# Forming the token-shifted inputs on two engines, and those of the second stream inside its low-rank loop

## The chip, the cores and the metric

The kernel runs on one core of a Trainium2 chip. A core has engines that run side by side, each in the order of its own queue: the matrix engine TensorE (PE in the profile), VectorE (DVE), ScalarE (ACT), GpSimd (POOL) and SyncE (SP), which here issues most of the DMAs. The metric is device microseconds (us) of one execution, as the median of several runs; a change is judged by the ratio of the two kernels' times.

## The reference

Two layers are applied to two streams of 512 tokens by 1024 features, with shared weights: first an RWKV-7 block (a linear recurrence, run forward and backward), then neighbourhood attention on a grid. The change touches the inputs of the first block. Cut to that:

```
xx = 0.5 * (x_prev + x_next) - xn            # tokens t-1 and t+1, zeros at the ends
lerp = lambda j: xn + xx * mu[j]
r, k, v = lerp(0) @ w_r, lerp(1) @ w_k, lerp(2) @ w_v
z = xn @ w_z
for d in range(2):
    w_log = -softplus(-(w0[d] + tanh(lerp(3 + d) @ w1[d]) @ w2[d])) - 0.5
    a = sigmoid(a0[d] + (lerp(5 + d) @ a1[d]) @ a2[d])
    ...                                      # scan of direction d with r, k, v, w_log, a
```

The matrices w1 and a1 have 64 columns each, so four narrow products of 1024 x 64 stand beside the wide ones. Everything is fp32.

## The kernel before

Activations lie transposed: 128 features on the partitions, 512 tokens along them, so one stream is KT = 8 tiles of 128x512. A fp32 matrix product is made of three matmuls on rounded halves: each operand is split into `hi` (a cast on ACT) and `lo` (a subtraction on DVE), by `halves`, L377 and L378, and `gemm` issues hi·hi, hi·lo and lo·hi for each of 8 tiles (L428 to L430). A column is 128 output features: 24 matmuls, after which ACT evicts the sum.

Work is in two parts. In the prelude, up to about 170 us, the code of `prelude(0)`, `prelude(1)` and the columns of z and k of stream 0 is interleaved, and a scheduler with its own estimates of durations sets the order of instructions on every engine. From then on (`scan_phase`), orders come from a planner written for this kernel, which puts instructions down one after another: weights of further columns are split at L730 and L732, their products are L811 to L813, and the low-rank weights and gates of the scan are prepared (L863 to L904) for the scans themselves. On every engine instructions run in their order, and a waiting one holds up those behind it.

What `prelude(s)` does for a stream: loads the eight tiles, makes their sum of squares, the reciprocal root (`rstds`, L461 to L470, with a matmul against ones that spreads it over the partitions) and the normed tiles `xn`. Then it forms `xx` in two DVE instructions for each tile, L541 and L542. The loop over k at L549 to L561 multiplies the normed tiles with the four narrow matrices, as they stand (`ps`) and multiplied by their mu (`pm`), twelve matmuls a tile (L558 to L560); the shift by a token is made afterwards on the small products (L569 to L579), which become four hidden activations (L581, of 64 rows: two with tanh). For stream 0 they stay on the chip; for stream 1 each is saved to memory (`save("hid")`). The tiles `lm` and `lr` of that part have a single buffer each. After it come the shifted inputs, a lerp by one DVE instruction a tile: v of stream 0, and k, r and v of stream 1, 32 tiles in all at L590, each saved to memory for later columns. They use the pool tag "ls" with four buffers, as do `hi` and `lo` of stream 1 in the loop over k. The inputs k and r of stream 0 are made by `shifted` (L608, 16 tiles) and split at once for the columns.

`save` (L327) and `load` (L333) both issue on SP in this part. Memory tensors are named in the orders by a leading d: dlk, dlr and dlv are shifted inputs, dhid hidden activations, dss the sums of squares of k, which are saved, loaded in another shape and made into the factors drn (L669 to L672). `rb` and `k` are the first tiles of the scan's preparation, loaded on SP; L863 on DVE multiplies them, L865 and L867 split the low-rank weights, and L882 on PE is the first product with these. `cv` holds the given vectors, `dv` vectors derived from them once, at the start, in `consts`.

Of the kernel before, what the change touches and what calls it, by code (L numbers as in the profile page):

```python
# [11 lines left out]
F32 = mybir.dt.float32  # L12
F32R = mybir.dt.float32r
AF = mybir.ActivationFunctionType
ALU = mybir.AluOpType
# [4 lines left out]
P = 128  # L20
T = 512
# [210 lines left out]
class Trunk:  # L232
# [110 lines left out]
    def consts(self):  # L343
        nc, cp = self.nc, self.cp
        self.cc = cp.tile([P, NCC], F32, tag="cc", name="cc")
        nc.sync.dma_start(self.cc, self.a["const"])
        c = lambda n, w: self.cc[:, CC[n]:CC[n] + w]
        self.ident, self.bones, self.ssel = c("ident", 128), c("bones", 128), c("ssel", 2)
        if self.SUMS:
            self.bones = cp.tile([P, 128], F32R, tag="sel", name="sel")  # L350
            nc.scalar.copy(self.bones, c("bones", 128))
        self.mstrict, self.mr = c("mstrict", 64), (c("mr", 64), self.cc[:, CC["mr"] + 64:CC["mr"] + 128])
        self.scan = (c("scan", T), self.cc[:, CC["scan"] + 1:CC["scan"] + 1 + T])
        w = c("win", 64)
        self.lower = bass.AP(tensor=w.tensor, offset=w.offset + 31, ap=[list(w.ap[0]), [-1, 32], [1, 32]])
        self.ones = cp.tile([P, P], F32, tag="ones", name="ones")
        nc.vector.memset(self.ones, 1.0)
        self.one = self.ones[:, 0:1]
        self.dv = dv = cp.tile([P, 88], F32, tag="dv", name="dv")
        v = lambda n, w, o=0: self.cv[:, CV[n] + o:CV[n] + o + w]  # L360
        ts = nc.vector.tensor_scalar
        ts(dv[:, 0:32], v("w0", 32), 0.5, None, op0=ALU.mult)
        ts(dv[:, 32:40], v("ka", 8), 0.5, None, op0=ALU.mult)
        ts(dv[:, 40:48], v("ka", 8), -0.5, 1.0, op0=ALU.mult, op1=ALU.add)
        ts(dv[:, 48:56], v("bin", 8), 0.125, None, op0=ALU.mult)
        ts(dv[:, 56:64], v("bin", 8, 24), 0.5, None, op0=ALU.mult)
        ts(dv[:, 64:72], v("bin", 8, 16), 0.5, None, op0=ALU.mult)
        ts(dv[:, 72:80], v("lnw", 8), 0.5, None, op0=ALU.mult)
        ts(dv[:, 80:88], v("lnb", 8), 0.5, None, op0=ALU.mult)

    def vec(self, n, i):
        return self.cv[:, CV[n] + i:CV[n] + i + 1]
# [127 lines left out]
    def prelude(self, s):  # L500
        nc = self.nc
        vt, gps, act = nc.vector, nc.gpsimd, nc.scalar
# [3 lines left out]
        for k in range(KT):  # L506
            if s == 0 and k == self.WFIRST:
                self.first = [self.weight(self.a["w_z"][0])]
            t = self.t("xn", (P, T + 2), 16, F32, self.lp)
# [21 lines left out]
        xn, xx = [], []  # L531
        for k, t in enumerate(xs):
            x = t[:, 1:T + 1]
# [5 lines left out]
        for k, t in enumerate(xs):  # L539
            u = self.t("xx", (P, T), 16, F32, self.lp)  # L540
            vt.tensor_tensor(u, t[:, 2:T + 2], t[:, 0:T], op=ALU.add)  # L541
            vt.scalar_tensor_tensor(u, u, 0.5, t[:, 1:T + 1], op0=ALU.mult, op1=ALU.subtract)  # L542
            xx.append(u)
            yield
        self.shift[s] = xn, xx

        pm = self.p("pf", (P, 2, T))
        ps = (self.p("pm"), self.p("us"))
        for k in range(KT):  # L549
            if s == 0:  # L550
                hi, lo = self.xz[k]
            else:
                hi, lo = (self.t("ls", (P, T), 4, F32R, self.lp) for _ in range(2))
                self.halves(xn[k], lo, hi, self.alt(k))
            for q2 in range(2):
                for out, w in ((pm[:, q2], self.wm), (ps[q2], self.wl)):
                    a, b = (m[:, k % 4] for m in w[2 * q2 + k // 4])
                    nc.tensor.matmul(out, a, hi, start=(k == 0), stop=False)  # L558
                    nc.tensor.matmul(out, a, lo, start=False, stop=False)
                    nc.tensor.matmul(out, b, hi, start=False, stop=(k == KT - 1))  # L560
                yield  # L561
        for q2 in range(2):
            mw = self.t("lm", (P, KT * P), 1, F32, self.lp)[:, 0:T + 2]
            lr = self.t("lr", (P, KT * P), 1, F32, self.lp)
            y, u = lr[:, 0:T], lr[0:64, T:2 * T]
# [18 lines left out]
                else:  # L584
                    self.save("hid", s, q, u)
            yield
        for kind, j in (("v", 2),) if s == 0 else (("k", 1), ("r", 0), ("v", 2)):
            for k in range(KT):
                t = self.t("ls", (P, T), 4, F32, self.lp)
                vt.scalar_tensor_tensor(t, xx[k], self.vec("mu", 8 * j + k), xn[k], op0=ALU.mult, op1=ALU.add)  # L590
                self.save("l" + kind, s, k, t)
                yield
        if s == 1:
            for k in range(KT):
# [2 lines left out]
    def hidden(self, q, u):  # L597
# [2 lines left out]
        self.nc.scalar.copy(h[0:64], u)  # L600
        self.nc.vector.tensor_tensor(h[64:128], u, h[0:64].bitcast(F32), op=ALU.subtract)

    def shifted(self, s, j):
        xn, xx = self.shift[s]

        def source(k):
            t = self.t("xr", bufs=self.NXR)
            self.nc.vector.scalar_tensor_tensor(t, xx[k], self.vec("mu", 8 * j + k), xn[k], op0=ALU.mult, op1=ALU.add)  # L608
            return t

        return self.operands(source)
# [1305 lines left out]
```

## Time and profile before

| | |
|---|---|
| median of 3 runs | 1658.08 us (1657.85 to 1667.48) |
| the profiled execution | 1657.03 us, span 1655.2 us |
| mean granted clock of PE | 0.974 |
| DVE instructions L542, busy | 10.0 us |
| DVE lerps L590 and L608, busy | 23.3 and 12.0 us |

A line of a group gives the line in the code, engine and operation, output and inputs, shape and count, then busy time and mean duration of one, then the engine's idle time just before them and what ended it. A line of the timeline gives the start and the duration in us; what stands in square brackets is the time that the engine had been idle and what ended that. A line of the waits gives the engine, the instruction, what it waited for, and the sum, the number and the longest of such waits. "zy", "pm", "pf" and "us" are accumulators of PE; "whi" and "wlo" halves of weights, "act" halves of inputs.

### The profile page before, as it was taken

To read this page: it belongs to the slowest core of one execution; us is meant where nothing else is said; L and a number is where in the kernel's file an instruction comes from. 1 tells how busy PE (TensorE), PEld (TensorE's weight loads), DVE (VectorE), ACT (ScalarE), POOL (GpSimd) and SP (SyncE) were. 2 spreads that over 40 slices of the span, in tenths; PEclk is the share of its full clock that TensorE was granted. 3 is DMA by queue.
4 is the path that set the end of the run, shared out by engine and by line. 5 is a ranking of instruction groups with operands and counts; after the bars stand their busy time and mean duration, and the time that the engine had idled before them with its cause. 6 is when DMAs were issued, how large, how long until landed. Compare 5 with 4: busy or idle time off the path is not lost.

```text
span 1655.2 us, 46478 instructions
## 1 busy us (share of the span) xinstructions
PE 1559.5 (94%) x18826; PEld 1197.2 (72%) x18826; DVE 1225.7 (74%) x2725; ACT 983.8 (59%) x1979; POOL 175.7 (11%) x334
## 2 busy tenths in 40 slices
PE   7989899998989998998988999999999999999998
PEld 6867667776667776776766777777777788777776
DVE  8995669688789787897888897865576585665564
ACT  5443566766756677665575665454567665455562
POOL 0000113311101224010000011000000002100000
PEclk9989999999999999999997999999999999999999
DMA  6435678776676787676777675554865346755553
GB/s 212 159 127 171 209 239 280 221 246 218 229 259 228 219 261 242 211 253 187 236 229 233 193 254 162 190 180 133 281 218 171 109 141 210 245 157 181 167 157 108
DMA packets 176312, 336.28 MB, mean 203 GB/s; under 512 B 20929, under 2 KB 53825, under 8 KB 176097
## 3 DMA queue, kind: packets, MB, share of 16 engines
q1 hardware_dynamic: 152800, 253.60, 48.2%
q0 software_dynamic: 23296, 79.71, 14.1%
q8 instruction: 148, 2.42, 0.6%
q14 instruction: 68, 0.55, 0.1%
HBM read 227.71 MB, written 105.51 MB: 201 GB/s over the span
## 4 chain that ended last, share of the span: by engine, by line
PE 49%; DVE 7%; ACT 5%; DMA 3%; issue 3%; POOL 0%; DVEq 0%; SPq 0%; ACTq 0%; POOLq 0%
PE pg L428 6%; PE pg L429 6%; PE pg L430 6%; PE pm L811 4%; PE pm L812 3%; PE pm L813 3%; PE sc L1437 2%; PE po L1470 2%; PE pf L1099 2%; PE pt L1455 2%; PE us L1218 1%; PE zy L1171 1%; PE us L1198 1%; PE zy L1222 1%; DVE ab L925 1%
## 5 line engine op out<-in xcount | busy, mean ns | idle before, releaser
L811 PE MATMUL pm<-act,whi 128*128 128x512 f32 x640 | 286.4, 447 | 12.2 <-ACT whi L730 4.9
L812 PE MATMUL pm<-act,whi 128*128 128x512 f32 x640 | 258.0, 403 | 10.2 <-DVE act L758 5.1
L813 PE MATMUL pm<-act,wlo 128*128 128x512 f32 x640 | 257.1, 402 | 6.0 <-DVE wlo L732 6.0
L811 PEld LDWEIGHTS pm<-act,whi 128*128 128x128 f32 x640 | 123.2, 192 | 55.3 <-issue 10.4
L377 ACT CAST whi<-raw 128x512 fp32r<-128x512 f32 x148 | 91.5, 618 | 118.3 <-PE pg L429 64.7
L428 PE MATMUL pg<-act,whi 128*128 128x512 f32 x384 | 158.5, 413 | 0.4 <-DVE tmp L1393 0.4
L429 PE MATMUL pg<-act,whi 128*128 128x512 f32 x384 | 152.5, 397 | 0.0
L430 PE MATMUL pg<-act,wlo 128*128 128x512 f32 x384 | 152.2, 396 | 0.0
L812 PEld LDWEIGHTS pm<-act,whi 128*128 128x128 f32 x640 | 123.8, 193 | 36.1 <-DVE act L758 14.9
L813 PEld LDWEIGHTS pm<-act,wlo 128*128 128x128 f32 x640 | 123.3, 193 | 36.0 <-DVE wlo L732 9.0
L378 DVE TENSOR_TENSOR wlo<-raw,whi 128x512 fp32r<-128x512 f32 x148 | 101.6, 688 | 58.8 <-ACT whi L377 56.5
L732 DVE TENSOR_TENSOR wlo<-raw,whi 128x512 fp32r<-128x512 f32 x160 | 109.1, 685 | 36.4 <-ACT whi L730 36.1
L730 ACT CAST whi<-raw 128x512 fp32r<-128x512 f32 x160 | 98.0, 617 | 41.2 <-PE pm L812 21.8
L428 PEld LDWEIGHTS pg<-act,whi 128*128 128x128 f32 x384 | 72.3, 188 | 15.6 <-issue 3.3
L430 PEld LDWEIGHTS pg<-act,wlo 128*128 128x128 f32 x384 | 72.3, 188 | 14.9 <-issue 0.3
L429 PEld LDWEIGHTS pg<-act,whi 128*128 128x128 f32 x384 | 72.4, 189 | 13.9 <-issue 2.5
L1003 DVE TENSOR_TENSOR etmp<-N 128x30 f32<-128x30 f32 (+14 forms) x240 | 78.6, 328 | 4.3
L1005 DVE TENSOR_TENSOR N<-etmp,N 128x30 f32<-128x30 f32 (+14 forms) x240 | 78.8, 328 | 4.0
L1448 DVE CUSTOM_DVE_ANT_0 sb<-sc,bias 128x256 f32<-128x256 f32 x128 | 49.2, 419 | 28.0 <-PE pt L1455 20.4
L1451 ACT ACTIVATE sb<-sb,mx 128x256 f32<-128x256 f32 x128 | 64.0, 502 | 6.8 <-DVE mx L1450 6.5
L1099 PE MATMUL pf<-cab 64*64 64x128 f32 (+1 forms) x2048 | 66.2, 266 | 0.4 <-issue 0.3
L1210 ACT COPY X<-us 64x256 f32<-64x256 f32 x128 | 46.9, 366 | 26.2 <-PE zy L1077 22.2
(403 smaller groups left out, 3636.2 us busy)
## 6 DMA issues: line engine op xcount, KB each, us to landing
dab<-ab POOLq DMA_DIRECT2D x32, 1024.0 KB, 7.1
cab<-dab SPq DMA_DIRECT2D x64, 512.0 KB
raw<-in_w_in_dram SPq DMA_DIRECT2D x128, 256.0 KB
bias<-in_rpb_dram SPq DMA_DIRECT2D x32, 384.0 KB
raw<-in_w_z_dram SPq DMA_DIRECT2D x32, 256.0 KB
raw<-in_w_k_dram SPq DMA_DIRECT2D x32, 256.0 KB
raw<-in_w_r_dram SPq DMA_DIRECT2D x32, 256.0 KB
k<-dk SPq DMA_DIRECT2D x32, 256.0 KB
```

The lines of the kernel that those rows point to most:

```text
L377: self.nc.scalar.copy(hi, src)
L378: (eng or self.nc.vector).tensor_tensor(lo, src, hi.bitcast(F32), op=ALU.subtract)
L428: nc.tensor.matmul(ps, hi, x[k][0], start=(k == 0), stop=False)
L429: nc.tensor.matmul(ps, hi, x[k][1], start=False, stop=False)
L430: self.mm = nc.tensor.matmul(ps, lo, x[k][0], start=False, stop=(k == KT - 1))
L730: nc.scalar.copy(hi, raw[h])
L732: nc.vector.tensor_tensor(lo, raw.pop(h), hi.bitcast(F32), op=ALU.subtract)
L811: nc.tensor.matmul(ps, hi[:, at], xh, start=(k == 0), stop=False)
L812: nc.tensor.matmul(ps, hi[:, at], xl, start=False, stop=False)
L813: nc.tensor.matmul(ps, lo[:, at], xh, start=False, stop=(k == KT - 1))
L1005: vt.tensor_tensor(N[:, q + 1:, :q], tv, N[:, q + 1:, :q], op=ALU.add)
L1099: end = nc.tensor.matmul(st.f[half(a), h, 0, d, g] if st.last else st.f[half(a), h, :, d, g], ab[half(h), d, g, 2 * e[d] + 1 - a], rt if s ...
```

## The change

Three things are done. L542 goes, so that `xx` is the plain sum of the neighbours. The lerp, xn + mu (0.5 sum - xn), is written as (1 - mu) xn + (0.5 mu) sum: ACT multiplies xn by a scale for each partition (1 - mu), and DVE adds the sum times 0.5 mu, in a new function `lerp` that all 48 tiles use. The factors are two more derived vectors. And the 24 shifted inputs of stream 1 are formed inside the loop of the narrow products, three after the products of each tile, where they stood after the hidden activations.

```
+        ts(dv[:, 88:112], v("mu", 24), 0.5, None, op0=ALU.mult)
+        ts(dv[:, 112:136], v("mu", 24), -1.0, 1.0, op0=ALU.mult, op1=ALU.add)
...
             vt.tensor_tensor(u, t[:, 2:T + 2], t[:, 0:T], op=ALU.add)
-            vt.scalar_tensor_tensor(u, u, 0.5, t[:, 1:T + 1], op0=ALU.mult, op1=ALU.subtract)
...
+        def mixed(kind, j, k):
+
+            t = self.t("ls", (P, T), 4, F32, self.lp)
+            self.lerp(t, xn[k], xx[k], 8 * j + k)
+            self.save("l" + kind, s, k, t)
...
                     nc.tensor.matmul(out, b, hi, start=False, stop=(k == KT - 1))
+                yield
+            for kind, j in (("k", 1), ("r", 0), ("v", 2)) if s else ():
+                mixed(kind, j, k)
                 yield
...
-        for kind, j in (("v", 2),) if s == 0 else (("k", 1), ("r", 0), ("v", 2)):
+        if s == 0:
             for k in range(KT):
-                t = self.t("ls", (P, T), 4, F32, self.lp)
-                vt.scalar_tensor_tensor(t, xx[k], self.vec("mu", 8 * j + k), xn[k], op0=ALU.mult, op1=ALU.add)
-                self.save("l" + kind, s, k, t)
+                mixed("v", 2, k)
                 yield
...
+    def lerp(self, t, x, u, i):
+
+        self.nc.scalar.activation(t, x, AF.Identity, scale=self.dv[:, 112 + i:113 + i])
+        self.nc.vector.scalar_tensor_tensor(t, u, self.dv[:, 88 + i:89 + i], t, op0=ALU.mult, op1=ALU.add)
...
             t = self.t("xr", bufs=self.NXR)
-            self.nc.vector.scalar_tensor_tensor(t, xx[k], self.vec("mu", 8 * j + k), xn[k], op0=ALU.mult, op1=ALU.add)
+            self.lerp(t, xn[k], xx[k], 8 * j + k)
             return t
```

Lines move by up to 13: L377 and L378 of before are L379 and L380, L558 to L560 are L565 to L567, L581 is L591 and L608 is L613 on ACT with L614 on DVE, L669 is L682, L730 is L743, L863 is L876, L882 is L895. Order changes in the prelude alone; behind it every engine has the same instructions in the same order. On PE both kernels have the same products, but the eight steps of stream 1's narrow products, which were over in the fourth column of k, now reach to the end of the last.

ACT around the last split inputs of k of stream 0 (`act` from `xr`), up to the square root of stream 1's norm (`rs`), before:

```order
L377 CAST act_927<-xr_924 128x512
L377 CAST whi_1121<-raw_1117 128x512
L377 CAST act_933<-xr_930 128x512
L377 CAST act_939<-xr_936 128x512
L377 CAST act_945<-xr_942 128x512
L377 CAST act_1641<-xr_1638 128x512
L461 ACT_TABLE_LOAD
L461 ACTIVATE rs_859<-pm_854,eps 128x4
```

and after, without the first rows: ahead of these stand the same cast of weights (now `whi_1112`), a cast to `act` and an activation of `lr` at L591:

```order
L379 CAST act_941<-xr_937 128x512
L608 CAST h_137_663<-lr_651 64x512
L379 CAST act_948<-xr_944 128x512
L613 ACTIVATE xr_951<-xn_137,dv 128x512
L613 ACTIVATE xr_1664<-xn_83,dv 128x512
L591 ACTIVATE lr_651<-lr_651 64x512
L608 CAST h_138_667<-lr_651 64x512
L613 ACTIVATE xr_1671<-xn_89,dv 128x512
L379 CAST act_955<-xr_951 128x512
L379 CAST act_1668<-xr_1664 128x512
L463 ACT_TABLE_LOAD
L463 ACTIVATE rs_861<-pm_856,eps 128x4
```

Between the cast of weights and the table load stood four casts, and now stand seven casts and five activations, three of them new lerps.

ACT at the end of the prelude, where the factors of k are made (`tmp`, from dss, by a square root) and the scan's first weights are split, before:

```order
L658 COPY tmp_1628<-pm_1626 2x512
L377 CAST act_1677<-xr_1674 128x512
L581 ACTIVATE lr_1297<-lr_1297 64x512
L669 ACT_TABLE_LOAD
L669 ACTIVATE tmp_1631<-tmp_1631 128x64
L377 CAST act_1683<-xr_1680 128x512
L756 CAST act_1732<-xr_1715 128x512
L730 CAST whi_1744<-raw_1723 128x512
L730 CAST whi_1764<-raw_1742 128x512
L581 ACTIVATE lr_1297<-lr_1297 64x512
```

and after:

```order
L743 CAST whi_1798<-raw_1776 128x512
L682 ACT_TABLE_LOAD
L682 ACTIVATE tmp_1657<-tmp_1657 128x64
L591 ACT_TABLE_LOAD
L591 ACTIVATE lr_1543<-lr_1543 64x512
L581 COPY lm_1562<-pf_1051 128x512
L591 ACTIVATE lr_1543<-lr_1543 64x512
L655 COPY tmp_1812<-pm_1768 128x512
L743 CAST whi_1836<-raw_1796 128x512
L591 ACTIVATE lr_1563<-lr_1563 64x512
L655 COPY tmp_1858<-pm_1808 128x512
L591 ACTIVATE lr_1563<-lr_1563 64x512
```

Of the four hidden activations of stream 1, two stood earlier and two around the square root; now all four come behind it, the first with a table load of its own, and the last cast of weights of the second column stands behind the second.

SP at the same place, with the saves of hidden activations (dhid) and the first loads of the scan's preparation (`rb`, `k`), before:

```order
L327 DMA dhid_299_1308<-lr_1297 64x512
L333 DMA xr_1729<-dlv_142_688 128x512
L333 DMA xr_1754<-dlv_144_695 128x512
L333 DMA drn_411_1636<-tmp_1631 128x64
L333 DMA xr_2244<-dlv_146_702 128x512
L333 DMA raw_1797<-in_w_r_dram 128x512
L327 DMA dhid_300_1311<-lr_1297 64x512
L333 DMA raw_1839<-in_w_r_dram 128x512
L333 DMA rb_1788<-drn_411_1636 64x512 x2
L333 DMA k_1786<-dk_234_1002 128x512
```

and after:

```order
L327 DMA dhid_379_1554<-lr_1543 64x512
L333 DMA drn_411_1662<-tmp_1657 128x64
L327 DMA dhid_380_1557<-lr_1543 64x512
L333 DMA tmp_1828<-in_lora_dram 128x512
L333 DMA raw_1900<-in_w_r_dram 128x512
L327 DMA dhid_383_1574<-lr_1563 64x512
L327 DMA dhid_384_1577<-lr_1563 64x512
L333 DMA rb_1822<-drn_411_1662 64x512 x2
L333 DMA k_1820<-dk_234_1008 128x512
```

The loads of `rb` and `k` stand behind all four saves, each of which waits for its activation.

More of the change, by code (lines that the diff above doesn't have):

```diff
@@ L358, in consts @@
         self.one = self.ones[:, 0:1]
-        self.dv = dv = cp.tile([P, 88], F32, tag="dv", name="dv")
+        self.dv = dv = cp.tile([P, 136], F32, tag="dv", name="dv")
         v = lambda n, w, o=0: self.cv[:, CV[n] + o:CV[n] + o + w]
```

## The prediction

> **What bounds the kernel now.** I read the page first, then the busy time by stretches of the part of the program that the change touches, then what the matmul engine waited for there, then the timeline of the two places where those waits lie. The page gives the whole:
>
> ```profile
> span 1655.2 us, 46478 instructions
> PE 1559.5 (94%) x18826; PEld 1197.2 (72%) x18826; DVE 1225.7 (74%) x2725; ACT 983.8 (59%) x1979; POOL 175.7 (11%) x334
> ```
>
> PE is busy for 94% of the span, so work taken from DVE or put on ACT counts only where PE waits for one of them. Everything that the diff edits runs in the first 170 us or so. The stretches there (start:end, busy us and count of PE, weight loads, DVE, ACT, POOL, then granted clock, DMA share, GB/s) and PE's waits up to 210 us (us in all, times, longest):
>
> ```profile
> 60.00:80.00 20.00, 20.00 (x90) 16.55 (x89) 18.28 (x31) 12.14 (x22) 0.13 (x2) 1.00 0.58 190
> 80.00:100.00 20.00, 14.28 (x48) 10.06 (x48) 19.76 (x36) 12.11 (x20) 0.13 (x2) 0.68 0.20 58
> ...
> 120.00:140.00 20.00, 20.00 (x83) 14.50 (x82) 4.75 (x8) 5.80 (x10) 0.00 (x0) 1.00 0.20 67
> ...
> 160.00:180.00 20.00, 15.09 (x58) 9.68 (x57) 17.25 (x28) 11.95 (x21) 0.00 (x0) 0.98 0.75 255
> 180.00:200.00 20.00, 18.01 (x70) 13.56 (x70) 9.25 (x16) 11.38 (x22) 4.87 (x6) 0.93 0.58 178
> ```
>
> ```profile
> PE pm L811 <- ACT whi L730: 3.7, 2, 2.6
> PE zy L429 <- DVE act L378: 3.5, 3, 2.3
> ...
> PE pm L470 <- DVE tmp L466: 2.3, 1, 2.3
> ```
>
> From 60 to 100 us DVE is full (18.28 and 19.76 of 20) and ACT has 8 us in 20 to spare. From 80 to 100 PE is the one that waits, for DVE: 3.5 + 2.3 = 5.8 us, and its clock was granted at 0.68, so that of 20 us about 2 x 0.32 x 20 = 12.8 ran at half speed, which cost half of them, 6.4 us. From 120 to 140 PE is full and neither DVE nor ACT matters. The third place is the join of the prelude and the scan, 160 to 200.
>
> **Shifted inputs, cheaper on DVE, dearer on ACT.** The groups of before (line, engine, operation, count, then busy us and mean ns):
>
> ```profile
> L590 DVE SCALAR_TENSOR_TENSOR ls<-xx,cv,xn 128x512 f32<-128x512 f32 x32 | 23.3, 751 | 6.5 <-DMA dlr<-ls 2.7 <-PE us L559 2.2 <-DMA dlk<-ls 1.5
> ...
> L542 DVE SCALAR_TENSOR_TENSOR xx<-xx,xn 128x512 f32<-128x512 f32 x16 | 10.0, 688 | 0.0
> ...
> L515 ACT ACTIVATE act<-xn,cv 128x512 fp32r<-128x512 f32 x8 | 5.6, 713 | 0.0
> ```
>
> Removed: 16 x 0.688 = 11.0 us of DVE, half of it (stream 0) in the full stretch before 98 us. The 48 lerps keep one DVE instruction each of the same kind (751 ns). Added: 48 x 0.713 = 34.2 us of ACT, the price of the nearest ACT row, Identity with a scale per partition on the same shape. The two DVE instructions on 128x24 elements stand where the kernel's vectors are made; each is a twentieth as wide as the rows of 0.69 and costs less than that: nothing on PE's path.
>
> How the full stretch ends, before:
>
> ```profile
> 75.26 0.62 ACT L377 CAST whi<-raw 128x512 fp32r<-128x512 f32 x1 [0.53 <-PE zy L429]
> 75.79 0.62 ACT L600 CAST h<-lr 64x512 fp32r<-64x512 f32 x1
> ...
> 83.70 0.62 ACT L377 CAST whi<-raw 128x512 fp32r<-128x512 f32 x1 [0.77 <-PE zy L429]
> ...
> 92.08 1.28 ACT L461 ACT_TABLE_LOAD   x1
> 93.37 0.26 ACT L461 ACTIVATE rs<-pm,eps 128x4 f32<-128x4 f32 x1
> ```
>
> ```profile
> 94.39 0.18 DVE L463 RECIPROCAL rs<-rs 128x4 f32<-128x4 f32 x1
> ...
> 96.81 2.04 PE L470 MATMUL pm<-tmp,ones 128*128 128x128 f32 x8 [2.26 <-DVE tmp L466]
> ```
>
> The cast of the weights at 83.70 waits for PE, not for ACT, and I keep its time. Behind it before had four casts, spread to 92 us by waits for DVE. After has twelve more instructions up to the table load (seven casts, five activations), and DVE is no longer late for them: 83.70 + 7 x 0.53 (the distance of two casts) + 5 x 0.71 + 0.62 = 91.6 for the end of the last operand, then 1.28 of table load and 0.26 of square root: 93.1, reciprocal 0.18, scaling of the identity, and PE some 0.5 later, at 93.8, where it was at 96.81. Three DVE instructions stood between reciprocal and scaling before; the new order has none. **Term 1: -3.0 us.** Bounds: 0, if ACT with its 24 more instructions up to here (17 us into some 16 us of room since 60) gets to the cast at 83.70 late; -12.2, if all of the wait and the half clock (5.8 + 6.4) go. I take the chain, since each link has a row. ACT replaces DVE as what PE waits for here, so most of the clock stays low.
>
> **Stream 1's lerps within the low-rank loop.** Rows of the loop's start, of stores on the shared buffers, and of saving hidden activations:
>
> ```profile
> 106.28 0.39 PE L558 MATMUL pf<-ls,lw 128*128 128x512 f32 x1
> ```
>
> ```profile
> 144.47 0.98 SPq L327 DMA_DIRECT2D dlk<-ls  x2
> ```
>
> ```profile
> 146.62 2.74 DVE L590 SCALAR_TENSOR_TENSOR ls<-xx,cv,xn 128x512 f32<-128x512 f32 x4 [1.52 <-DMA dlk<-ls]
> ```
>
> ```profile
> 157.39 0.53 SPq L327 DMA_DIRECT2D dhid<-lr  x1
> ```
>
> ```profile
> 161.72 0.63 ACT L581 ACTIVATE lr<-lr 64x512 f32<-64x512 f32 x1 [3.39 <-DMA dhid<-lr]
> ```
>
> Four buffers now hold five tiles a step. A buffer stored at 144.47 could be written again at 146.62: 2.2 us. That of 157.39 was free at 161.72, 4.3 us, with some 0.3 from the end of the writer to the issue 4.6. I take the middle, s = 3.4, as the stores now go out in both kinds of stretch. The ring of the new program is: lerp k waits for the products of the step before, v for the store of k, the next r for the store of v, the next cast for the store of r. Three steps so hold three lerps with their stores, one cast, one subtraction and one step's products among columns (22 matmuls in the new order, at 20.0 / 83 = 0.24 us by the stretch from 120 to 140: 5.3): (3 x (0.71 + 0.75 + s) + 0.62 + 0.69 + 5.3) / 3 = 5.9 us a step at s = 2.2, 7.1 at 3.4, 8.3 at 4.6. PE needs (167.2 - 106.3) / 8 = 7.6 us a step for the loop and the k columns beside it, whose number of matmuls is unchanged. **Term 2: 0**, hidden under PE's columns; at s = 4.6 the cover is gone and it costs 8 x 0.7 = 5.6 us. Below nothing it hardly comes: none of PE's waits is on a product of this loop.
>
> Queued behind a lerp that waits on ACT stand the casts of weights and the evictions of k columns; PE is the one that would wait for them, which is the same cost. The 24 stores are not new; they come from behind the loop into it, where the DMA share was 0.20 between 120 and 140.
>
> **The tail.** In before the loop ended early among the columns, and two of its four hidden activations were made by 157 and 162 us. Now the last low-rank product is the last but one thing before the scan's columns, and all four come after it, on single buffers.
>
> ```profile
> 166.80 0.39 PE L430 MATMUL zy<-act,wlo 128*128 128x512 f32 x1
> ```
>
> ```profile
> 171.87 0.57 ACT L658 COPY tmp<-pm 2x512 f32<-2x512 f32 x1
> ...
> 175.20 0.63 ACT L581 ACTIVATE lr<-lr 64x512 f32<-64x512 f32 x1 [0.64 <-DVE lr L579]
> 176.06 1.28 ACT L669 ACT_TABLE_LOAD   x1 [0.23 <-DMA tmp<-dss]
> ```
>
> ```profile
> 176.20 0.46 SPq L327 DMA_DIRECT2D dhid<-lr  x1
> ...
> 180.90 0.45 SPq L327 DMA_DIRECT2D dhid<-lr  x1
> 181.40 0.58 SPq L333 DMA_DIRECT2D raw<-in_w_r_dram  x1
> ...
> 183.25 0.58 SPq L333 DMA_DIRECT2D k<-dk  x1
> ```
>
> ```profile
> 188.08 0.75 DVE L863 SCALAR_TENSOR_TENSOR rb<-k,cv,rb 128x512 f32<-128x512 f32 x1 [2.01 <-DMA k<-dk]
> ...
> 190.70 0.69 DVE L867 TENSOR_TENSOR w2l<-tmp,w2h 128x512 fp32r<-128x512 f32 x1 [1.87 <-ACT w2h L865]
> ```
>
> ```profile
> 191.45 0.50 PE L882 MATMUL pm<-h,w2l 128*128 128x512 f32 x1 [0.23 <-DVE w2l L867]
> ```
>
> The loop ends on PE at 167.2, the last k column nine products (2.2 us) earlier, so the copy of its sum of squares ends at 172.4 - 2.2 = 170.2. Its way through memory took 172.4 to 176.1, 3.6: 173.8. In the new order ACT then has table load, square root, a second table load, first hidden activation: 1.28 + 0.26 + 1.28 + 0.63, 177.3. Store (s), second activation 0.63, store, since DVE writes the next pair into the same buffer: 184.7; three DVE instructions of 0.69: 186.8; third copy and its store: 190.8; fourth copy: 191.5; its issue 0.4 later (175.8 to 176.2): 191.9. On SP the loads of the scan's first k stand behind it, before 2.35 from one issue to the other with a weight's load between, 0.7, that now stands elsewhere: 193.5. Landing as before, 188.1 - 183.3 = 4.8: 198.3. DVE in order: that product and the weights' low part, 0.75 each, then PE at 199.8, where it was at 191.45. **Term 3: +8.4**, passed on whole, as from there both engines' orders are written out. Three round trips stand in it, so its bounds are +4.8 at s = 2.2 (+2.2 if k also lands in 2.2, as the store did) and +12.0 at 4.6.
>
> Meanwhile PE has run out of columns, at about the 191 of before, and its clock falls:
>
> ```profile
> 179.60 0.79 PE L811 MATMUL pm<-act,whi 128*128 128x512 f32 x1 [2.64 <-ACT whi L730]
> ...
> 182.76 0.39 PE L812 MATMUL pm<-act,whi 128*128 128x512 f32 x1
> ```
>
> After 2.64 us of waiting seven matmuls took 3.2 us, where seven at 0.24 take 1.7: **term 4: +1.5**, from nothing, if this stretch waits for other engines anyway, to twice that. [...]
>
> [...]
>
> **Sum.** 1657.0 (profiled execution, its span 1655.2 and 1.8 around it) - 3.0 + 0 + 8.4 + 1.5 = 1663.9, and as the median of before is 1658.1, 1.05 above that execution, 1665.
>
> **Rivals.** First, the gain is all there is: freed of DVE, PE loses all 5.8 us of waits and half of the 6.4 at half clock, and the tail costs its least, +2.2: 1657.0 - 9.0 + 2.2 + 1.05 = 1651. For it: DVE is 19.76 of 20 there, and 144.47 shows a quick store. Against it: ACT gets 24 instructions in the same 40 us, and the chain of four stores is in the order, whatever each costs. Second, on the side of slower: the stores' round trips become the pace of the low-rank loop. With s at 5 the ring takes 8.7 us a step, 1.1 x 8 = 8.5 more, the tail +13.2: 1657.0 - 3.0 + 8.5 + 13.2 + 1.5 + 1.05 = 1678. It passes 1% from s = 4.7 on. For it: 4.6 has been seen, with a DMA share of 0.75, and the ring has no spare buffer; against it: in 120 to 140 the DMA share was 0.20, and the other store took 2.2. Third, that nothing follows: ACT's room swallows its instructions, the tail's chain is hidden by other loads that were late anyway: 1658.
>
> **Chances and range.** A measurement of this kernel tells about 1%, 16.6 us, from no change. Forecast (1655 to 1674) 0.55, first rival 0.20, ring 0.20, third 0.05. More than 1% faster needs the whole first stage and no tail: 0.03 of the first rival. The ring is slower by over 1% in most of its cases, with a little of the forecast's upper end: 0.20. That leaves 0.77 within. The range goes from 1649, the first rival and a little less tail, to 1679, the ring at s = 5.
>
> **What would show it.** Right: DVE's share in 80 to 100 falls, PE's matmul on the scaled identity starts 2 to 4 us earlier, PE is full from 104 to 164, four saves of hidden activations follow each other from 177 on at 4 us, and the first product of the scan's low-rank weights starts 5 to 12 us later. Wrong: PE waits for casts of the low-rank loop, or the load of the scan's first k goes out well ahead of the fourth save. The forecast falls if PE waits on the loop by more than 5 us, or if what comes after 200 us has slack that takes the delay back.

## The result, and the profile after

| | before | changed |
|---|---|---|
| median of 12 runs | 1658.40 us (1655.71 to 1668.76) | 1657.99 us (1654.73 to 1666.13) |
| the profiled execution | 1657.03, span 1655.2 | 1659.26, span 1657.5 |
| ratio changed to before | | 0.9991, 95% interval 0.9977 to 1.0005 |

The time did not change by more than the runs can tell: -1.5 us by the ratio, with zero inside its interval. The forecast was 1665 and no change. The stretches of the changed kernel (start:end, busy us and count of PE, weight loads, DVE, ACT, POOL, then granted clock, DMA share, GB/s):

```profile
80.00:100.00 20.00, 15.76 (x58) 12.00 (x57) 19.18 (x35) 17.52 (x28) 0.13 (x2) 0.74 0.26 79
...
120.00:140.00 20.00, 20.00 (x79) 13.54 (x79) 11.10 (x16) 13.17 (x23) 0.00 (x0) 1.00 0.54 187
...
160.00:180.00 20.00, 19.82 (x82) 14.67 (x82) 11.97 (x21) 13.99 (x23) 0.80 (x3) 1.00 0.56 162
180.00:200.00 20.00, 11.43 (x41) 8.75 (x40) 8.98 (x15) 9.64 (x19) 4.25 (x5) 0.74 0.37 120
```

What PE waited for up to 230 us (us in all, times, longest):

```profile
PE pm L895 <- DVE w2l L880: 4.3, 1, 4.3
PE pm L894 <- ACT w2h L878: 4.3, 1, 4.3
PE zy L431 <- DVE act L380: 3.2, 2, 3.1
PE pm L824 <- ACT whi L743: 1.2, 2, 1.1
PE zy L430 <- ACT act L379: 1.0, 1, 1.0
PE pm L472 <- DVE tmp L468: 0.3, 1, 0.3
```

From 160 to 180 PE is busy for 19.82 of 20 us, where before it was for 15.09; from 180 to 200 it has 11.43, where it had 18.01. The same work moved to the front, and a wait of 4.3 + 4.3 us came behind it. PE's timeline at the marks that the prediction named, the scaled identity, the end of the low-rank loop, the first column of r, the first product with w2l and the scan's first small matmuls, and, between the first two, at the end of the column behind the identity (L668, the sum of squares of a column of k):

```profile
95.34 1.77 PE L472 MATMUL pm<-tmp,ones 128*128 128x128 f32 x8
...
101.82 1.02 PE L668 MATMUL pm<-tmp,cc 128*2 128x512 f32 x2
...
165.45 0.39 PE L567 MATMUL us<-ls,lw 128*128 128x512 f32 x1
165.77 1.02 PE L668 MATMUL pm<-tmp,cc 128*2 128x512 f32 x2
166.72 2.86 PE L1641 MATMUL zy<-cc 128*128 128x256 f32 x12
169.22 0.58 PE L824 MATMUL pm<-act,whi 128*128 128x512 f32 x1
...
186.80 0.80 PE L894 MATMUL pm<-h,w2h 128*128 128x512 f32 x1 [4.26 <-ACT w2h L878]
191.91 0.80 PE L895 MATMUL pm<-h,w2l 128*128 128x512 f32 x1 [4.31 <-DVE w2l L880]
...
202.29 0.86 PE L973 MATMUL pf<-ab 64*32 64x64 f32 x64
```

The rows of before for the end of that column, for the first column of r and for the scan, with two waits ahead of the scan (the prediction shows the identity's row, 96.81, and w2l's, 191.45):

```profile
104.53 1.02 PE L655 MATMUL pm<-tmp,cc 128*2 128x512 f32 x2
...
173.87 0.58 PE L811 MATMUL pm<-act,whi 128*128 128x512 f32 x1
...
197.58 0.50 PE L811 MATMUL pm<-act,whi 128*128 128x512 f32 x1 [1.09 <-ACT whi L730]
...
198.98 0.50 PE L813 MATMUL pm<-act,wlo 128*128 128x512 f32 x1 [0.67 <-DVE wlo L732]
...
203.99 0.86 PE L960 MATMUL pf<-ab 64*32 64x64 f32 x64
```

So the changed kernel is 1.5 us ahead at 95, 2.7 at the end of the column behind it (the same place in PE's order in both kernels), 4.7 at the first column of r, 0.5 behind at w2l, and 1.7 ahead as the scan starts. From there both run the same order, and the profiled execution of the changed kernel still ended 2.3 us later than that of before. Over the fourteen profiles here (before, changed, and twelve experiments, by span less that mark) the rest of the program took between 1446 and 1468 us, with no relation to when it began. One execution's total thus does not show 2 us; the marks before the scan do.

### The profile page after: what moved, and what is told of

The parts are those of the page before. It is cut to its first block, busy times and chain, and to the rows that moved or that the text cites. A ratio compares the mean times of both kernels' runs of the same rounds, so it can differ in the third digit from the quotient of the medians.

```text
span 1657.5 us, 46539 instructions
## 1 busy us (share of the span) xinstructions
PE 1557.6 (94%) x18826; PEld 1197.0 (72%) x18826; DVE 1217.3 (73%) x2711; ACT 1013.8 (61%) x2027; POOL 175.8 (11%) x334
## 4 chain that ended last, share of the span: by engine, by line
PE 47%; DVE 8%; ACT 5%; DMA 4%; issue 3%; SPq 0%; POOL 0%; DVEq 0%; ACTq 0%; POOLq 0%
PE pg L430 6%; PE pg L431 6%; PE pg L432 6%; PE pm L824 4%; PE pm L825 3%; PE pm L826 3%; PE pf L1112 2%; PE sc L1450 2%; PE po L1483 2%; PE pt L1468 2%; PE us L1231 1%; PE zy L1184 1%; PE us L1211 1%; PE zy L1235 1%; DMA raw<-in_w_in_dram 1%
## 5 line engine op out<-in xcount | busy, mean ns | idle before, releaser
L379 ACT CAST whi<-raw 128x512 fp32r<-128x512 f32 x148 | 91.3, 617 | 106.5 <-PE pg L431 68.7
L380 DVE TENSOR_TENSOR wlo<-raw,whi 128x512 fp32r<-128x512 f32 x148 | 101.4, 687 | 60.9 <-ACT whi L379 60.2
L743 ACT CAST whi<-raw 128x512 fp32r<-128x512 f32 x160 | 97.8, 617 | 42.0 <-PE pm L825 24.3
L1135 DVE TENSOR_TENSOR AK<-zy,cc 128x256 f32<-128x256 f32 x63 | 26.6, 422 | 52.0 <-PE zy L1090 51.9
```

What stands on the lines that cost most here:

```text
L379: self.nc.scalar.copy(hi, src)
L380: (eng or self.nc.vector).tensor_tensor(lo, src, hi.bitcast(F32), op=ALU.subtract)
L743: nc.scalar.copy(hi, raw[h])
```

## The experiments

Times of the marks in us, each from one profiled execution; medians and ratios are each against runs of before on the same chip. "Split" is the lerp on two engines, "fused" that on DVE alone.

| kernel | lerp, place of stream 1's | identity | loop's last product | w2l | scan begins | ratio to before, 95% |
|---|---|---|---|---|---|---|
| before | fused, behind | 96.8 | 147.2 | 191.5 | 204.0 | 1 |
| changed | split, in loop | 95.3 | 165.5 | 191.9 | 202.3 | 0.9991 (0.9977 to 1.0005) |
| split_behind | split, behind | 94.6 | 139.0 | 189.0 | 201.6 | 1.0000 (0.9982 to 1.0018) |
| fused_in_loop | fused, in loop | 96.4 | 167.8 | 197.6 | 208.8 | 1.0016 (1.0001 to 1.0030) |
| hid_buffers | split, in loop | 94.7 | 165.9 | 186.3 | 196.5 | 0.9977 (0.9957 to 0.9997) |
| v_in_tmp | split, in loop | 95.2 | 158.1 | 185.9 | 196.8 | 0.9975 (0.9951 to 0.9998) |
| v_in_tmp_hid | split, in loop | 94.9 | 158.1 | 186.2 | 197.1 | 0.9975 (0.9953 to 0.9996) |
| fused_cured | fused, in loop | 96.0 | 164.6 | 189.0 | 200.3 | 0.9997 (0.9981 to 1.0013) |
| split_behind_hid | split, behind | 94.9 | 139.0 | 195.2 | 207.7 | 1.0032 (1.0013 to 1.0050) |
| sums_on_pool_cured | split, in loop | 95.0 | 162.7 | 186.9 | 197.9 | 0.9982 (0.9963 to 1.0001) |
| ring3 | split, in loop | 94.7 | 177.8 | 201.9 | 213.2 | one run, 1675.2 us |
| sums_on_pool | split, in loop | 94.9 | 172.3 | 197.9 | 208.1 | one run, 1669.8 us |
| no_act | split without ACT's half, in loop | 94.6 | 161.4 | 187.4 | 198.9 | one run, 1653.7 us |
| no_adds | split, in loop | (moved) | 165.4 | 193.5 | 204.4 | one run, 1669.8 us |

Over the ten kernels with ratios a line through the ratios against the start of the scan has a slope of 0.66 us of time for 1 us of start, with a correlation of 0.94: most of what is gained or lost before the scan arrives at the end, within what the runs can tell.

**One part at a time.** First the split lerps alone, with stream 1's behind the hidden activations as before; then the placement alone, with the fused lerp and the second instruction on the sum.

```
# split_behind: in the changed kernel
-            for kind, j in (("k", 1), ("r", 0), ("v", 2)) if s else ():
-                mixed(kind, j, k)
-                yield
...
-        if s == 0:
+        for kind, j in (("v", 2),) if s == 0 else (("k", 1), ("r", 0), ("v", 2)):
             for k in range(KT):
-                mixed("v", 2, k)
+                mixed(kind, j, k)
# fused_in_loop: in the changed kernel
             vt.tensor_tensor(u, t[:, 2:T + 2], t[:, 0:T], op=ALU.add)
+            vt.scalar_tensor_tensor(u, u, 0.5, t[:, 1:T + 1], op0=ALU.mult, op1=ALU.subtract)
...
-        self.nc.scalar.activation(t, x, AF.Identity, scale=self.dv[:, 112 + i:113 + i])
-        self.nc.vector.scalar_tensor_tensor(t, u, self.dv[:, 88 + i:89 + i], t, op0=ALU.mult, op1=ALU.add)
+        self.nc.vector.scalar_tensor_tensor(t, u, self.vec("mu", i), x, op0=ALU.mult, op1=ALU.add)
```

> The lerps on two engines as in the changed kernel, but stream 1's 24 stand behind the hidden activations again, as before. Theory (two separate effects: DVE relieved is worth 1.5 us by 95 us, the loop's placement nets about nothing at the join of prelude and scan): PE's matmul on the scaled identity at 95.3 us (before 96.8, changed 95.3), low-rank products over early, the first product with w2l at about 190 (before 191.45), the scan's first small matmuls (64x64, 64 of them) at about 202.5 (before 204.0, changed 202.3); ratio to before 0.999. Rival (what is ahead at the scan comes from the placement): the same 95.3, but the scan's first matmuls at 203.5 to 204.5, ratio 1.000.

> The lerps on DVE alone as before (with the second DVE instruction on the neighbours' sum), formed inside the low-rank loop as in the changed kernel. Theory of two effects: identity matmul at 96.8 us, the loop's last product at about 167.3 (changed: 165.5), the first column of r begins 1.4 us later than in the changed kernel, at 170.6, and the scan's first small matmuls at 203.8; ratio to before 1.000. Rival (placement gives the lead): scan's first matmuls at 202.3, ratio 0.999. A third way: DVE, with 5.5 us more work, makes PE wait in the loop: PE's waits between 106 and 167 of 2 us or more, ratio above 1.002.

The split alone brought the identity to 94.6 and the scan to 201.6, 2.4 us ahead of before; the time stayed at 1.0000 within 0.18%. The first theory holds for it. The placement alone was worse than either theory: PE had no wait in the loop, and the identity and the loop's end came where they were put (96.4 and 167.8), but w2l stood at 197.6 and the scan began at 208.8, 4.8 us behind before, with a ratio just above 1. PE's waits in that kernel, from its timeline:

```profile
191.79 0.50 PE L894 MATMUL pm<-h,w2h 128*128 128x512 f32 x1 [1.33 <-ACT w2h L878]
197.59 0.79 PE L895 MATMUL pm<-h,w2l 128*128 128x512 f32 x1 [5.30 <-DVE w2l L880]
```

So the placement does have a price at the join, 6.1 us at w2l by this kernel. But the two parts do not add up, against the theory of two separate effects: 2.4 us of gain and 4.8 of loss would leave the changed kernel 2.4 behind at the scan, and it is 1.7 ahead. Of the 6.5 us between fused_in_loop and the changed kernel there, 2.4 are there at the end of the column behind the identity (104.3 against 101.8). Later the last column's sum of squares took 6.6 us on its way through memory in place of 4.1 (from the end of ACT's copy at 170.3 to 176.9), and a table load stood behind it, not ahead. Why its way took longer was not tested.

**The chain of saves.** The four hidden activations of stream 1 get tiles of their own from the tag ls, so that nothing waits for a save. The same was done to the kernel with the lerps behind.

```
# hid_buffers: in the changed kernel; split_behind_hid: the same edit in split_behind
             for q in (2 * q2, 2 * q2 + 1):
+                if s:
+                    u = self.t("ls", (P, T), 4, F32, self.lp)[0:64]
                 act.activation(u, y[64 * (q % 2):64 * (q % 2) + 64], AF.Tanh if q < 2 else AF.Copy)
```

> The changed kernel, with the four hidden activations of stream 1 written into tiles of the four-buffer tag ls, so that none waits for the save of the one before. Theory (three round trips of saves stand in the chain to the scan's first k): the fourth save is issued at about 178 us (changed: 185), k's load at 180 (186.9), the first product with w2l at 184.8 (191.9), PE's waits ahead of the scan fall from 8.6 to 2 us or less, the scan's first small matmuls at about 195 (202.3); ratio to before 0.996. Rival (another load is late next, such as weights of r): w2l's product at 185 but the scan's first matmuls at 199 or later, ratio 0.998.

> Lerps on two engines, those of stream 1 behind the hidden activations as before, and the hidden activations in tiles of ls. Theory (the chain of saves matters only where the loop ends late): nothing gained over the same placement without them: PE's first product with w2l at 188.5 to 189.5 (189.0), scan's first small matmuls at 201 to 202 (201.6), ratio to before 0.999 to 1.000. Rival (single buffers of the hidden activations cost time in any placement): scan's first matmuls at 199 or earlier.

In the changed kernel the edit moved w2l from 191.9 to 186.3 and the scan from 202.3 to 196.5. The queue of SP in the changed kernel and in this one:

```profile
173.72 0.54 SPq L327 DMA_DIRECT2D dhid<-lr  x1
174.34 0.53 SPq L333 DMA_DIRECT2D drn<-tmp  x1
176.82 0.47 SPq L327 DMA_DIRECT2D dhid<-lr  x1
...
182.12 3.43 SPq L327 DMA_DIRECT2D dhid<-lr  x2
185.66 1.18 SPq L333 DMA_DIRECT2D rb<-drn  x2
186.89 0.58 SPq L333 DMA_DIRECT2D k<-dk  x1
```

```profile
173.77 1.16 SPq L327 DMA_DIRECT2D dhid<-ls  x2
...
177.89 1.10 SPq L327 DMA_DIRECT2D dhid<-ls  x2
179.91 0.33 SPq L333 DMA_DIRECT2D raw<-in_w_r_dram  x1
180.34 1.11 SPq L333 DMA_DIRECT2D rb<-drn  x2
181.50 0.58 SPq L333 DMA_DIRECT2D k<-dk  x1
```

The first save goes out at the same time in both; k's load, behind the fourth, goes out 5.4 us earlier. That is the chain, shown by taking it away. The size fell short of what was expected by 1.5 us, since k's load now stands behind a weight's load.

With the lerps behind, the edit was expected to do nothing, and made the scan begin 6.1 us later (207.7), and the kernel slower by 0.32%. The theory had looked at the saves alone. With four more tiles in the ring ls the lerps come later (the last starts on ACT at 181.1 us, in split_behind at about 170), and ACT forms their first halves in the very stretch in which it must evict the last column of k. From PE's timeline:

```profile
170.59 1.87 PE L667 MATMUL pm<-tmp,cc 128*2 128x512 f32 x2 [5.17 <-ACT tmp L663]
...
182.88 0.75 PE L823 MATMUL pm<-act,whi 128*128 128x512 f32 x1 [3.08 <-ACT whi L742]
```

5.17 us of wait for an eviction, and 3.08 for a cast of weights, both queued on ACT behind lerps; ACT had no gap of more than 0.3 us there from 161 to 181. In split_behind the same wait for the eviction was 3.8, in before 2.3, and in the changed kernel there is none: nine products of the loop stand between the last column and that matmul and cover it. That is what forming the lerps in the loop is worth on its good side.

**The ring of four buffers.** Three buffers in place of four; and, the other way, the lerps of v in another tag, so that the ring has four tiles a step on four buffers. This second was run without and with the tiles for the hidden activations.

```
# ring3: in the changed kernel, here and where the loop takes hi and lo
-            t = self.t("ls", (P, T), 4, F32, self.lp)
+            t = self.t("ls", (P, T), 3, F32, self.lp)
# v_in_tmp: in the changed kernel; v_in_tmp_hid: in hid_buffers
-            t = self.t("ls", (P, T), 4, F32, self.lp)
+            t = self.tmp() if s and kind == "v" else self.t("ls", (P, T), 4, F32, self.lp)
```

> The changed kernel with three buffers in place of four in the tag ls. Theory (the ring of four took about 6 us a step where PE needs 7.6, so its stores were covered with 1.7 us a step to spare): with three buffers two stores stand one behind the other in each step, PE waits in the loop for 4 to 15 us in all, and the scan begins that much later, single time 1660 to 1675. Rival (the stores were never near the path): PE waits under 1 us in the loop and the time is within the spread of the changed kernel, 1655 to 1662.

> The changed kernel, with the lerps of v of stream 1 in buffers of another tag (tmp, five buffers), so that the ring ls holds four tiles a step on four buffers; hidden activations still on single buffers. Theory (the ring does not stall PE but sets where the scheduler can put the loop's products, and the scan waits for the loop's end plus a chain of some 25 us): the loop's last product at 158 to 162 us (changed: 165.5), PE's two waits of 4.3 us ahead of the scan shrink to under 3 together, the scan's first small matmuls at 195 to 199 (202.3, before 204.0), ratio to before 0.996 to 0.998. Rival (the end of the loop is not what the scan waits for, the columns of r are): scan's first matmuls at 201 or later, ratio 0.999 or above.

> Both: lerps of v in tag tmp, hidden activations of stream 1 in tiles of ls, so that no save is waited for. Theory: loop's end at 158 to 162 us, the four saves out before 176, nothing of them left on the way to the scan, PE is held by its columns of r alone: first product with w2l at 184 to 187, scan's first small matmuls at 194 to 197, about what the hidden tiles alone gave (196.5): the two cures remove the same wait, not two. Rival (they add up): below 192. Ratio to before 0.996 to 0.998.

With three buffers PE did not wait in the loop at all, as the rival had it and the theory had not; yet the time went up, against the rival, in its one run. The scheduler, which reckons with the ring, had put the columns of r ahead (the first at 164.0) and the loop's end behind (177.8), and then PE ran dry:

```profile
PE pm L894 <- ACT w2h L878: 14.3, 1, 14.3
...
PE pm L895 <- DVE w2l L880: 4.6, 1, 4.6
```

So the ring's pace does cost, but not where the prediction looked for it: by the order that the scheduler made, it sets where the loop ends. The wider ring says the same from the other side: the loop's last product at 158.1, PE's wait ahead of w2l down from 8.6 to 0.2 us, the scan at 196.8. With the tiles for the hidden activations as well it was 197.1. The two cures remove the same wait, as expected, and do not add up. What is left is PE's own work: between the last product of r's columns and w2l it waits for 0.23 us.

```profile
167.57 0.94 PE L668 MATMUL pm<-tmp,cc 128*2 128x512 f32 x1 [2.45 <-ACT tmp L664]
...
185.87 0.50 PE L895 MATMUL pm<-h,w2l 128*128 128x512 f32 x1 [0.23 <-DVE w2l L880]
```

These two rows are of v_in_tmp: with the loop's end moved forward the wait for the last eviction is back, 2.45 us, the price of the cover lost. Hid_buffers, v_in_tmp and v_in_tmp_hid are the fastest of the kernels with a ratio, 0.23 to 0.25% below before, each with its interval below 1; against the changed kernel (0.9991) their intervals overlap, and the difference rests on the marks.

**The lerp's form with the join cured.** As v_in_tmp_hid, with the fused lerp and the second instruction on the sum (the edit of fused_in_loop).

> The lerps on DVE alone as before, but in the loop, with the lerps of v in tag tmp and the hidden activations in tiles of ls. Theory (the two engines' lerp and the placement are separate effects of about 1.5 to 2.5 us and of the join): identity matmul at 96.4 to 96.8 us, scan's first small matmuls 1.5 to 2.5 us behind those of the same kernel with lerps on two engines, at 198.5 to 199.7 (197.1; before 204.0); ratio to before 0.997 to 0.999. Rival (with the join cured the lerp's form makes no difference to it): 197 to 198; a third way (the fused lerp in the loop delays the join by itself, as the 208.8 of that placement without the cures may say): 202 or later.

The identity came at 96.0, the scan at 200.3, 3.2 us behind the same kernel with the split lerp: 0.6 past the first theory's range, with a ratio of 0.9997 where 0.999 was its upper end, and short of the third way's 202. Of the 3.2 us, 1.1 are there at the identity and 3.0 at the end of the column behind it (104.4 against 101.5). So the fused lerp in the loop delays the join by little of its own once the chain is gone; what it costs is lost in front.

**What holds PE up to 95 us.** The prediction had ACT take DVE's place there. Four kernels asked: the seven additions of stream 1's sum of squares on POOL (also in the cured kernel), the additions left out, and ACT's half of the lerps left out.

```
# sums_on_pool: in the changed kernel; sums_on_pool_cured: in v_in_tmp_hid
-            self.sumsq(acc, t[:, 1:T + 1], k, vt if s or k % 2 else vt)
+            self.sumsq(acc, t[:, 1:T + 1], k, gps if s else vt)
# no_adds: in the changed kernel, for stream 1
-            (eng or nc.vector).tensor_tensor(acc, sq, acc, op=ALU.add)
# no_act: in the changed kernel
-        self.nc.scalar.activation(t, x, AF.Identity, scale=self.dv[:, 112 + i:113 + i])
-        self.nc.vector.scalar_tensor_tensor(t, u, self.dv[:, 88 + i:89 + i], t, op0=ALU.mult, op1=ALU.add)
+        self.nc.vector.scalar_tensor_tensor(t, u, self.dv[:, 88 + i:89 + i], x, op0=ALU.mult, op1=ALU.add)
```

> The changed kernel, with the seven additions of stream 1's sum of squares on GpSimd (POOL) in place of VectorE. Theory (in the stretch up to 95 us DVE is still what PE waits for, ACT is not): DVE loses 7 x 0.69 = 4.8 us there and PE's matmul on the scaled identity comes 1.5 to 4 us earlier, at 91.5 to 94 us (changed: 95.3). Rival (ACT's chain of casts and lerps holds it, or POOL is too slow for the sums): at 95 us or later, with PE's wait before it ended by ACT or POOL.

> The kernel with lerps of v in tag tmp and hidden activations in tiles of ls, and the additions of stream 1's squares on POOL. Theory as for the additions alone: identity matmul at 91.5 to 94 us (94.9 without), and as PE has no wait behind it that would take the lead back, the scan's first small matmuls as much earlier, at 193.5 to 196 (197.1); ratio to before 0.993 to 0.997. Rival: the loop's end, which the new order puts 13 rows later on PE, comes to the front, and the scan's first matmuls stay at 197 or later.

> The changed kernel with the seven DVE additions of stream 1's sum of squares left out (the norm is made of one tile's squares; the squares themselves are still formed on ACT). Theory (DVE is still what PE waits for up to 95 us): identity matmul 1.5 to 4 us earlier, 91.5 to 94 (changed: 95.3), as 7 x 0.69 = 4.8 us of DVE are gone and none is slowed. Rival (ACT's chain, which took 31 of 40 us from 60 to 100): 95 or later.

> The changed kernel with ACT's half of all 48 lerps left out (DVE adds the scaled sum to xn itself, so the factor 1 - mu is missing); DVE's instructions are the same. Theory (DVE is still the bound up to 95 us, ACT's lerps are hidden): identity matmul at 94.5 to 95.8 (changed: 95.3). Rival (ACT has become the bound there, as the prediction had it): 93.5 or earlier.

Without ACT's half the identity stood at 94.6, within 0.7 us of the changed kernel: what ACT does of its halves by then (34 us over all 48 lerps) is hidden there, and at the end of the column behind the identity this kernel, at 102.1, was not ahead at all. PE's waits in that kernel from 84 to 90 us were still for DVE (2.45 and 0.16 us), and the next, 2.02 us for a cast on ACT, came after ACT itself had been idle for 4.32 us, waiting for a lerp on DVE. On POOL the additions gained nothing (94.9 and 95.0), though they left DVE, because DVE's instructions beside them took longer (1.45 to 1.77 us in place of 0.69), as the last section shows; the theory's numbers were missed, and the run can't decide between theory and rival. In the new order the loop also ended later (172.3 against 165.5), and the scan began 5.8 us later. Without the additions the scheduler moved the identity forward among PE's products, to 83.2 us, so that this mark compares with nothing; PE then waited 3.66 us for DVE at 94.2, with DVE busy for 19.87 of 20 us. That ACT's halves of the lerps do not hold the stretch is shown by no_act; that DVE does is read from what PE waits for, there and in the others. That a DVE with still less to do would give more was not shown.

## Why the prediction came out as it did

The verdict, no change, was right, and the time lies in the range; the forecast's 7 us above before were not there. This says little for the mechanism: a range from 1649 to 1679 holds a gain of 9 us as well as a loss of 20, and the time came out at 1658 because a gain in front and a loss at the join, both smaller than forecast, nearly cancel. Of the signs that the prediction named, PE was full from 104 to 164, and k's load stood behind four saves; the identity came 1.5 us earlier, not 2 to 4, w2l 0.5 later, not 5 to 12, and DVE's busy time from 80 to 100 fell by 0.58 us alone. By its own terms:

- **Term 1, -3.0 us at the scaled identity: right sign, half the size there.** Measured 96.81 - 95.34 = 1.5 (1.5 to 2.2 over the kernels with the split lerp that have the identity at this place of PE's order). The step that failed is that ACT replaces DVE as what PE waits for. DVE stayed full (19.18 of 20) and its in-order queue set the last operands; the 3.1 us of PE's longest wait is for DVE. The low clock stayed for the most part as forecast, 0.74 after 0.68 (in before PE's rows of 128x512 were of 0.63 us, 0.43 apart, in place of 0.39 and 0.23, from 88.3 to 100.8, 12.5 us where the forecast reckoned 12.8 at half speed; in the changed kernel from 88.2 to 96.9), but not to the end: behind the identity PE was back at 0.39 us a row from 97.2, where before it was from about 101. That made the lead 2.7 us at the end of the column, close to the forecast's 3.0 by a step that it did not have. At this place the seven kernels with the split lerp and the same order lie between 101.5 and 102.3 us, the three with the fused lerp between 104.3 and 104.5.
- **Term 2, 0 in the low-rank loop: right.** PE has no wait between 95 and 177 us in the changed kernel. Unforeseen was a gain: PE's 2.27 us for the last eviction went, since the loop's last nine products cover it, so that the columns of r began 4.7 us earlier. In them all but 0.18 of the 2.64 us for a cast of weights went too, and the slow rows after it (of 0.63 us, 0.43 apart, from 179.6 to 182.8 in before), and they ended 8.3 us earlier (the small products behind them begin at 181.1 against 189.4). It bought nothing by itself, as PE then waited 4.3 + 4.3 us for the chain.
- **Term 3, +8.4 at w2l: the mechanism right, the size wrong, and this is the step that decided.** The chain of four saves is there, k's load stands behind it, and taking it away brought 5.8 us. From the forecast's 199.8, less term 1, 196.8 was to be expected; 191.9 was measured, so that the term was +3.5 and not +8.4. The three round trips took 2.4 us each, end of one activation to the next instruction, where the middle of two rows, 3.4, had been taken: 3 us. k landed 3.6 us after its issue, not 4.8: 1.2 us. And the table load ahead of the square root did not wait for the data. In before the wait stood on the table load itself (176.06, 0.23 us idle); in the changed kernel it stands on the instruction behind:

```profile
168.98 1.28 ACT L682 ACT_TABLE_LOAD   x1
171.49 0.26 ACT L682 ACTIVATE tmp<-tmp 128x64 f32<-128x64 f32 x1 [1.23 <-DMA tmp<-dss]
171.76 1.28 ACT L591 ACT_TABLE_LOAD   x1
173.06 0.63 ACT L591 ACTIVATE lr<-lr 64x512 f32<-64x512 f32 x1
...
176.16 0.63 ACT L591 ACTIVATE lr<-lr 64x512 f32<-64x512 f32 x1 [2.00 <-DMA dhid<-lr]
```

  so 1.3 us more were saved. Of these 5.5 us, 0.7 were lost again ahead of the square root, since the sum of squares came back from memory at 171.5, where 173.8 - 3.0 was forecast; the other steps differ by 0.1. That leaves the 4.9.
- **"Passed on whole": wrong by 2 us.** Before lost 1.09 and 0.67 us between w2l and the scan to a cast of weights that was not ready, and had rows of 0.63 us in place of 0.39 there from 199.8 to 203.2; 12.5 us lie between the two marks. In the changed kernel, where PE had waited longer, that cast was ready, and 10.4 lie between them. Part of the delay fell on a wait that was there already. Before also had a table load of ACT in this stretch, which the changed kernel does not have, as it had done it ahead of the first hidden activation (171.76):

```profile
191.73 1.28 ACT L885 ACT_TABLE_LOAD   x1
```

  How much of the 2 us this makes was not tested.
- **Term 4, +1.5 for the low clock: there, and no longer apart.** After the wait PE ran at about half speed from 191.9 to about 195.5 (rows of 0.63 us, 0.43 apart, where they are of 0.39 and 0.23 apart at full speed), and before had its own such stretch from 199.8 to 203.2.

Of the rivals, the third (nothing follows, 1658, given 0.05) named the time that was measured, but by luck: ACT did take up its instructions, yet the tail's chain was not hidden, as the 8.6 us of waits show. The first (the gain is all there is, 1651) was as far off as the forecast, and neither its full clock nor its full gain came; the ring as the pace of PE did not happen with four buffers, nor with three.

## What to carry to other kernels

A change that gives an engine less to do is not worth the instructions removed, and when the engine stays full after it, it can stay the bound: 5.5 us of DVE were removed ahead of the identity here, and 1.5 came there, 2.7 once PE's clock was back. When work is moved into a loop, ask first what used to run while the loop was over: here four small results with a single buffer each, whose saves lay hidden, came to stand in line ahead of the next phase, and buffers of their own gave back 5.8 us. The scheduler here, which reckons with the buffer ring, did not let the matrix engine stall on it: it put the loop's end later, so with such a scheduler look for the price of a short ring behind the loop too, not only in it.

## What the runs showed of the hardware that was not expected

Additions of 128x512 on POOL took 1.47 us each, and DVE instructions beside them 1.45 to 1.77 us instead of 0.69. From the groups of POOL from 60 to 100 us, and the timelines of POOL and DVE, of sums_on_pool:

```profile
L445 POOL TENSOR_TENSOR acc<-tmp,acc 128x512 f32<-128x512 f32 x7 | 10.3, 1473 | 8.3 <-ACT tmp L444 8.0
```

```profile
73.07 4.69 POOL L445 TENSOR_TENSOR acc<-tmp,acc 128x512 f32<-128x512 f32 x3
80.85 2.99 POOL L445 TENSOR_TENSOR acc<-tmp,acc 128x512 f32<-128x512 f32 x2 [3.08 <-ACT tmp L444]
...
85.14 1.58 POOL L445 TENSOR_TENSOR acc<-tmp,acc 128x512 f32<-128x512 f32 x1
```

```profile
75.01 1.60 DVE L582 TENSOR_TENSOR lr<-lm 128x512 f32<-128x512 f32 x1
76.54 1.77 DVE L380 TENSOR_TENSOR wlo<-raw,whi 128x512 fp32r<-128x512 f32 x1
78.24 0.68 DVE L584 SCALAR_TENSOR_TENSOR lm<-lr,lm 128x512 f32<-128x512 f32 x1
...
81.24 1.45 DVE L380 TENSOR_TENSOR act<-xr,act 128x512 fp32r<-128x512 f32 x1
82.61 1.77 DVE L648 SCALAR_TENSOR_TENSOR tmp<-tmp,tmp 128x512 f32<-128x512 f32 x1
84.31 0.68 DVE L587 TENSOR_TENSOR lr<-lr,lm 128x512 f32<-128x512 f32 x1
...
85.51 1.77 DVE L380 TENSOR_TENSOR wlo<-raw,whi 128x512 fp32r<-128x512 f32 x1
```

The long ones lie in POOL's stretches and the short ones outside them, but for overlaps of under half a microsecond: the five long instructions of DVE here took 4.9 us longer in all, 0.82 for each of the six additions in POOL's rows, more than the 0.69 that DVE would take for it. Why they took longer was not tested.
